# Gate and up of a SwiGLU as seven half products (Strassen) for 16 of 22 tiles, the down projection in five groups, and weights halved 1024 wide

## The chip, the cores and the metric

The kernel runs on one core of one Trainium2 chip, in one launch. The metric is the device time in microseconds, the median of several runs. The engines of the core work side by side, each on its own queue in order: TensorE (PE) for matmuls into PSUM, with its weight loads (PEld), VectorE (DVE), ScalarE (ACT), GpSimd (POOL), and SyncE (SP), which issues the transfers.

## The reference

A trunk of two layers on a sequence of 512 tokens of 1024 features, float32. Each layer is a macaron:

```python
x = x + 0.5 * swiglu(rms_norm(x, ffn1_norm[i]), ...)      # width 2816
x = x + mixer(rms_norm(x, mix_norm[i]))                   # layer 0: block-sparse attention, layer 1: Mamba-2
x = x + 0.5 * swiglu(rms_norm(x, ffn2_norm[i]), ...)

def swiglu(x, w_gate, w_up, w_down):
    return (jax.nn.silu(x @ w_gate) * (x @ w_up)) @ w_down
```

So there are four SwiGLU blocks (FFNs 0 to 3) with gate and up of 1024 x 2816 and down of 2816 x 1024.

## The kernel before

Everything is kept transposed: `x` is eight tiles of 128 features x 512 tokens in SBUF, `h` (the hidden width) is 22 tiles of 128 x 512. Precision comes from halves: each operand a is split into a high part (rounded to the matmul's type by ScalarE, `high`) and a low part (a minus the high part, on VectorE, `low`), and each 128 x 128 block of a product is three matmuls, high by high, high by low, low by high (`mm3`). Names end in `hi` and `lo`: `whi`, `wlo` are halves of weights, `xhi`, `xlo` of the normed input, `hhi`, `hlo` of the hidden tiles.

Weights stream in through four raw buffers `wraw` of 128 x 2048 (1 MB), in the order of use. `halve_weights` cuts each into units of 512 columns and makes `whi` (ScalarE) and `wlo` (VectorE), with eight buffers of each kind; a unit is four 128 x 128 blocks, 12 matmuls of 512 columns.

An FFN (`ffn`) runs in two halves of 11 hidden tiles. In each half, for every tile j, a gate accumulation `pg` and an up accumulation `pu` over the eight tiles of x (48 matmuls, each in a PSUM bank of its own); then `gated` makes h from them: `pg` times the row norm `rb` (VectorE), silu (ScalarE), times `rb` (GpSimd), times `pu` (VectorE), and the halving of the result. After 11 tiles come eight down blocks `pd`, one for each tile of x, 33 matmuls each, and `residual` adds each to x on VectorE. The next stage's norm starts tile by tile as x is done (`Norm.add`): operands are scaled by the gain and halved at once, and the norm's row factor `rb` is applied later, in `gated`. The mixers use the same weights' machinery; in `wide`, used for q, k, v and z, two raw pieces (eight units) are held over two passes.

The order of work on all engines is not written by hand. A planner (`Scheduler`) runs the stages as tasks with its own costs for each operation; it issues next what could start first by its clock, with the priority as a tie break, so an instruction's place in its engine's queue is decided by these costs. The main task has the matmuls; the halving of weights is given as `EASY` work with a due time, and becomes `URGENT` when its due time is near (`pressing`). Buffers are pools (`slot` 128 x 512, `hs` 128 x 256, `ps` eight PSUM banks), given out by the planner.

Of the kernel before, what the change touches and what calls it, by code (L numbers as in the profile page):

```python
# [25 lines left out]
KT = D // 128  # L26
# [11 lines left out]


# [103 lines left out]
class Scheduler:  # L143
    def __init__(self, sizes):
# [3 lines left out]
        self.tag_of = {}  # L148
        self.written, self.read = {}, {}
# [82 lines left out]
    def release(self, tile):  # L232
        name = tile.tensor.name
        ends = [s[2] for book in (self.written, self.read) for s in book.pop(name, ())]
        room = self.room[self.tag_of.pop(name)]
        room.append(max(ends))
# [54 lines left out]
def trunk(ctx, tc, xT, pos, consts, cols, rows, wgu, wd, wqk, wv, wo, win, wz, wdt, wout, outT):  # L291
# [10 lines left out]
    sizes = {"slot": 48, "hs": 12, "sq": 6, "tiny": 40, "ps": 8, "wraw": 4, "whi": 8, "wlo": 8}  # L302
# [10 lines left out]
    raw_piece, hi_unit, lo_unit = room(wp, "wraw", 2048), room(wp, "whi", 512), room(wp, "wlo", 512)  # L313
# [24 lines left out]
    pieces = []  # L338

    def piece(src, n=2048, unit=2.73, total=None):  # L340


        pieces.append((src, n, unit, unit * n / 512 if total is None else total))

    def wide_pieces(w):
        piece(w[0], unit=1.36)
        piece(w[1], unit=1.36, total=16.4)

    for l in range(2):
        for i in (2 * l, 2 * l + 1):  # L350
            if i == 1:
                for what, c in ATTN:
                    if what == "wo":
                        piece(wo[c])
                    else:
                        wide_pieces(wqk[c] if what == "qk" else wv[c])
            if i == 3:
                piece(wdt, 256, total=5.5)
                for what, n in SSM:
                    if what == "x":  # L360
                        piece(win[n, 0])
                        piece(win[n, 1])
                    elif what == "z":
                        wide_pieces(wz[n])
                    else:
                        piece(wout[n, 0])
                        piece(wout[n, 1])
# [6 lines left out]
    needed = [0.0]  # L374
    for _, _, _, total in pieces:
        needed.append(needed[-1] + total)
    used = [0]

    def load_weights():
        for p in range(1, len(pieces)):  # L380
            src, n = pieces[p][:2]
            raw = yield raw_piece("wraw")
            yield SP.dma_start(raw[:, :n], src)
            raws[p], begun[p] = raw, n

    def halve_weights():
        for p in range(len(pieces)):
            n = pieces[p][1]
            cs = range(0, n, 512)
            for c in cs:  # L390
                at_work[:] = p, c
                yield When(lambda: begun.get(p, 0) > c)
                hi, lo = yield [hi_unit("whi", FR), lo_unit("wlo", FR)]
                w = min(512, n - c)
                yield high(raws[p][:, c:c + w], hi[:, :w])
                spawn(halve_low(p, c, w, hi, lo, c == cs[-1]), pressing(p, c))

    def halve_low(p, c, w, hi, lo, last):
        op = low(raws[p][:, c:c + w], hi[:, :w], lo[:, :w])
        yield op.frees(raws.pop(p)) if last else op  # L400
        units.setdefault(p, []).append((hi, lo))
# [3 lines left out]
    def pressing(p, c):  # L405

        due = needed[p] + c / 512 * pieces[p][2]
        return lambda: URGENT if due - Q.done_us < 6.0 else EASY + due

    def first_due():  # L410
        p, c = at_work
        return pressing(p, c)()
# [4 lines left out]
    def take(src):  # L417
        p = used[0]
        used[0] += 1
        assert pieces[p][0].offset == src.offset and pieces[p][0].tensor.name == src.tensor.name  # L420
# [753 lines left out]
```

## Time and profile before

| | us |
|---|---|
| median of 3 runs | 2116.16 (2116.1 to 2117.05) |
| the profiled execution | 2115.9 |
| its span on the core | 2113.9 |
| TensorE busy | 2106.1 |
| VectorE busy | 1117.0 |
| ScalarE busy | 877.6 |
| GpSimd busy | 400.4 |

How to read it: the span is the time from the first to the last instruction of the profiled execution, which is 0.3 us off the median of the runs. Busy time is the union of an engine's instructions. In the groups, a row has the line of the helper that records every operation (L214), the engine, the operation, output and inputs by the program's names, the shapes, the count, the busy time, the mean duration in ns of one, and the idle time of the engine before them with what ended it. A matmul's duration has its drain in it, which overlaps the next matmul; so its cost is the distance between starts. In windows, each engine has its busy time in that stretch and its number of instructions.

### The profile page before, as it was taken

What the parts mean: (1) busy time and instruction counts of PE and PEld (TensorE: products, weight loads), DVE (VectorE), ACT (ScalarE), POOL (GpSimd) and SP (SyncE); (2) the same over time, 40 slices, a digit from 0 to 9 for tenths busy, and PEclk for the clock granted to TensorE, in tenths of its full rate; (3) what the DMA queues carried; (4) which work ended last, traced back from release to release, by engine and by line L of the source; (5) the groups of instructions that cost most, each with busy time, mean ns of one, the idle gap of its engine ahead of it and who ended that gap; (6) DMA issues with size and microseconds to landing.
All of it is one profiled execution on the core that took longest, in us unless ns stands there. A gap on an engine that the chain in (4) does not pass through costs nothing.

```text
span 2113.9 us, 25353 instructions
## 1 busy us (share of the span) xinstructions
PE 2106.1 (100%) x9700; PEld 1748.7 (83%) x9700; DVE 1117.0 (53%) x1841; ACT 877.6 (42%) x1650; POOL 400.4 (19%) x377
## 2 busy tenths in 40 slices
PE   9999999999999999999999999999999999999999
PEld 7888888888888888888888888888888888888887
DVE  6444444668864434444443444677575774443442
ACT  5322334455443323333322334674747643322331
POOL 1101111332131001111100111244343442100100
PEclk9999999999999999999999999999999999999999
DMA  6223223212122232232232223233232332232221
GB/s 229 81 96 110 96 83 114 100 60 80 60 81 87 92 114 95 83 110 98 81 108 100 94 83 116 81 84 136 68 132 69 112 117 83 81 109 101 93 87 49
DMA packets 37129, 203.68 MB, mean 96 GB/s; under 512 B 4240, under 2 KB 4880, under 8 KB 19728
## 3 DMA queue, kind: packets, MB, share of 16 engines
q1 hardware_dynamic: 37008, 202.07, 27.9%
q8 instruction: 76, 1.25, 0.2%
q14 instruction: 45, 0.37, 0.1%
HBM read 199.89 MB, written 2.16 MB: 96 GB/s over the span
## 4 chain that ended last, share of the span: by engine, by line
PE 98%; DMA 1%; DVE 0%; ACT 0%; SPq 0%; POOL 0%; issue 0%; ACTq 0%; POOLq 0%
PE pd L214 23%; PE pu L214 22%; PE pg L214 22%; PE pin L214 8%; PE pqk L214 4%; PE pz L214 4%; PE pout L214 4%; PE pv L214 2%; PE pwo L214 2%; PE py L214 2%; PE psc L214 1%; PE pxt L214 1%; PE po L214 1%; PE pst L214 1%; PE ppt L214 0%; DMA wraw<-wgu 0%
## 5 line engine op out<-in xcount | busy, mean ns | idle before, releaser
L214 DVE TENSOR_TENSOR wlo<-wraw,whi 128x512 fp32r<-128x512 f32 (+1 forms) x737 | 555.3, 759 | 677.5 <-ACT whi L214 668.6
L214 ACT ACTIVATE whi<-wraw 128x512 fp32r<-128x512 f32 (+1 forms) x737 | 453.1, 619 | 778.7 <-PE pd L214 281.2
L214 POOL TENSOR_TENSOR ga<-ga,rb 128x512 f32<-128x512 f32 x88 | 114.1, 1298 | 977.8 <-ACT ga L214 575.0
L214 PE MATMUL pg<-xhi,whi 128*128 128x512 f32 x704 | 274.3, 390 | 1.2 <-ACT xhi L214 1.2
L214 PE MATMUL pg<-xlo,whi 128*128 128x512 f32 x704 | 274.2, 390 | 0.5 <-DVE xlo L214 0.5
L214 PE MATMUL pu<-xhi,whi 128*128 128x512 f32 x704 | 274.4, 390 | 0.0
L214 PE MATMUL pg<-xhi,wlo 128*128 128x512 f32 x704 | 273.9, 389 | 0.0
L214 PE MATMUL pu<-xhi,wlo 128*128 128x512 f32 x704 | 273.9, 389 | 0.0
L214 PE MATMUL pu<-xlo,whi 128*128 128x512 f32 x704 | 273.9, 389 | 0.0
L214 PE MATMUL pd<-hhi,whi 128*128 128x512 f32 x704 | 273.9, 389 | 0.0
L214 PE MATMUL pd<-hlo,whi 128*128 128x512 f32 x704 | 273.9, 389 | 0.0
L214 PE MATMUL pd<-hhi,wlo 128*128 128x512 f32 x704 | 273.9, 389 | 0.0
L214 PEld LDWEIGHTS pg<-xlo,whi 128*128 128x128 f32 x704 | 132.2, 188 | 29.0 <-DVE xlo L214 1.6
L214 PEld LDWEIGHTS pg<-xhi,whi 128*128 128x128 f32 x704 | 132.1, 188 | 28.9 <-ACT xhi L214 1.5
L214 PEld LDWEIGHTS pu<-xhi,wlo 128*128 128x128 f32 x704 | 132.2, 188 | 27.5
L214 PEld LDWEIGHTS pd<-hhi,wlo 128*128 128x128 f32 x704 | 132.1, 188 | 27.5
L214 PEld LDWEIGHTS pd<-hhi,whi 128*128 128x128 f32 x704 | 132.1, 188 | 27.4
L214 PEld LDWEIGHTS pu<-xhi,whi 128*128 128x128 f32 x704 | 132.2, 188 | 27.3
L214 PEld LDWEIGHTS pd<-hlo,whi 128*128 128x128 f32 x704 | 132.1, 188 | 27.4
L214 PEld LDWEIGHTS pg<-xhi,wlo 128*128 128x128 f32 x704 | 132.1, 188 | 27.3
L214 PEld LDWEIGHTS pu<-xlo,whi 128*128 128x128 f32 x704 | 132.1, 188 | 27.3
L214 ACT ACTIVATE hhi<-ga 128x512 fp32r<-128x512 f32 x88 | 55.6, 632 | 149.8 <-DVE ga L214 149.8
(211 smaller groups left out, 3036.4 us busy)
## 6 DMA issues: line engine op xcount, KB each, us to landing
wraw<-wgu SPq DMA_DIRECT2D x87, 1024.0 KB, 4.8
wraw<-wd SPq DMA_DIRECT2D x64, 704.0 KB, 4.1
wraw<-win SPq DMA_DIRECT2D x16, 1024.0 KB, 4.9
wraw<-wqk SPq DMA_DIRECT2D x8, 1024.0 KB, 4.9
wraw<-wz SPq DMA_DIRECT2D x8, 1024.0 KB, 4.9
rows_b<-rows_d SPq DMA_DIRECT2D x32, 256.0 KB, 5.5
wraw<-wout SPq DMA_DIRECT2D x8, 1024.0 KB, 4.8
wraw<-wv SPq DMA_DIRECT2D x4, 1024.0 KB, 4.8
```

The costliest lines, as they stand in the source:

```text
L214: op.fn(*op.args, **op.kw)
```

## The change

Six of the 22 hidden tiles stay as they were (`plain`), the other 16 are taken as 8 pairs. For a pair (j0, j1) the normed input is seen as a 2 x 2 matrix of blocks (A11, A12, A21, A22: tokens 0 to 255 and 256 to 511, features 0 to 511 and 512 to 1023) and the weights of the two tiles as another one (features by tile), and the four result blocks come from seven products in place of eight (Winograd's form of Strassen's scheme). Each product is 24 matmuls for gate and for up together: 4 blocks of features, three halves, twice, with 256 columns, gate in the left and up in the right half of one PSUM bank (`pp`). VectorE combines the products from PSUM (`c11`, `w_e`, `c12`, `c22`, `c21`), with the names `g1` to `g4`, and `gate` does the silu and the multiplication for 256 tokens.

The operands of the products are made in two places. `spread` makes the seven sums and differences of the normed input, once per FFN, with `rb` already applied (so in `gate` no factor `rb` is left and GpSimd has no part): `aa`, `ab`, `ad`, `ae` with their halves. `halve_pair` makes the seven sums of weights in place in the raw buffers (VectorE, 1024 columns: gate and up), and halves each.

The down projection goes by groups: (0, 6), (6, 10), (10, 14), (14, 18), (18, 22). Down blocks of a group are put among the pairs of the next group, four after each pair; each has 18 or 12 matmuls and its own `residual`. Weights are halved in units of 1024 columns, with four buffers of each kind; a unit that serves two accumulations is freed after both (`uses`).

```diff
+GROUPS = ((0, 6), (6, 10), (10, 14), (14, 18), (18, 22))
...
-    sizes = {"slot": 48, "hs": 12, "sq": 6, "tiny": 40, "ps": 8, "wraw": 4, "whi": 8, "wlo": 8}
+    sizes = {"slot": 55, "hs": 12, "sq": 6, "tiny": 40, "ps": 8, "wraw": 4, "whi": 4, "wlo": 4}
...
-    raw_piece, hi_unit, lo_unit = room(wp, "wraw", 2048), room(wp, "whi", 512), room(wp, "wlo", 512)
+    raw_piece, hi_unit, lo_unit = room(wp, "wraw", 2048), room(wp, "whi", 1024), room(wp, "wlo", 1024)
...
+    def ffn_order(i):
+
+        order = list(range(*GROUPS[0]))
+        for g in range(1, len(GROUPS)):
+            a, b = GROUPS[g]
+            pairs = [(j, j + 1) for j in range(a, b, 2)]
+            n = 0
+            for m, pair in enumerate(pairs):
+                order.append(pair)
+                while n < KT * (m + 1) // len(pairs):
+                    order.append(("down", g - 1, n))
+                    n += 1
+        return order + [("down", len(GROUPS) - 1, n) for n in range(KT)]
...
-            for hf in range(2):
-                for j in range(HALF):
-                    piece(wgu[i, hf * HALF + j])
-                for n in range(KT):
-                    piece(wd[i, hf, n], HALF * 128)
...
+            for c in range(0, n, 1024):
                 hi, lo = yield [hi_unit("whi", FR), lo_unit("wlo", FR)]
...
-                w = min(512, n - c)
+                w = min(1024, n - c)
...
+    def halve_pair(p, a, b):
+        a0, a1, b0, b1 = a[:, :1024], a[:, 1024:], b[:, :1024], b[:, 1024:]
+        plan = [(a0, None, []), (a0, b0, []), (a1, None, []), (a0, b1, []), (b1, None, []), (b0, b1, [b]), (a0, a1, [a])]
+        for m, (src, term, done) in enumerate(plan):
+            at_work[:] = p, m
+            if term is not None:
+                yield When(lambda: len(units[p]) == m)
+                yield V.tensor_tensor(src, src, term, op=OP.add)
+            hi, lo = yield [hi_unit("whi", FR), lo_unit("wlo", FR)]
+            yield high(src, hi)
+            spawn(halve_low(p, src, hi, lo, done), pressing(p, m))
...
-        return lambda: URGENT if due - Q.done_us < 6.0 else EASY + due
+        return lambda: URGENT if due - Q.done_us < 8.0 else EASY + due
...
+        def spread(self):
+            yield When(lambda: self.rb is not None)
+            rest = []
+            for k in range(4):
+                xa, xb = yield [slot("xa"), slot("xb")]
+                for t, kk in ((xa, k), (xb, k + 4)):
+                    op = V.scalar_tensor_tensor(t, x[kk], self.gain[:, kk:kk + 1], self.rb, op0=OP.mult, op1=OP.mult)
...
+                bh, bl, d = yield [slot("abhi", FR), slot("ablo", FR), slot("ad")]
+                yield high(xb, bh)
+                yield V.tensor_tensor(d[:, :256], xa[:, 256:], xb[:, 256:], op=OP.subtract)
+                yield low(xb, bh, bl)
+                yield V.tensor_tensor(d[:, 256:], xa[:, :256], d[:, :256], op=OP.subtract)
+                yield V.tensor_tensor(xb[:, :256], xb[:, :256], d[:, 256:], op=OP.subtract)
+                yield V.tensor_tensor(xb[:, 256:], xa[:, :256], xa[:, 256:], op=OP.subtract)
+                ah, al, dh, dl = yield [half_slot("aahi", FR), half_slot("aalo", FR), slot("adhi", FR), slot("adlo", FR)]
+                yield high(xa[:, :256], ah)
+                yield low(xa[:, :256], ah, al).frees(xa)
+                yield high(d, dh)
+                yield low(d, dh, dl).frees(d)
...
+            for k in range(4):
+                eh, el = yield [slot("aehi", FR), slot("aelo", FR)]
+                yield high(rest[k], eh)
+                yield low(rest[k], eh, el).frees(rest[k])
...
+            def product(m, name):
+                ps = yield bank("pp")
+                yield unit(p, m)
+                un = units[p][m]
+                for o in range(2):
+                    for k in range(4):
+                        yield When(lambda: nrm.left[name][k] is not None)
+                        ops = mm3(ps[:, 256 * o:256 * o + 256], cut(un, 512 * o + 128 * k, 512 * o + 128 * k + 128),
+                                  nrm.left[name][k], k == 0, k == 3)
+                        if o and k == 3:
+                            ops[-1].frees(*un)
+                        if last and o:
+                            ops[-1].frees(*nrm.left[name][k])
+                        yield ops
+                return ps
...
+            def gate(j, t, src):
+                if j not in out:
+                    out[j] = [None, 2]
+                    out[j][0] = yield slot("ga")
+                yield When(lambda: out[j][0] is not None)
+                a = out[j][0][:, 256 * t:256 * t + 256]
+                yield S.activation(a, src[:, :256], AF.Silu)
+                yield V.tensor_tensor(a, src[:, 256:], a, op=OP.mult).frees(src)
...
+            def c11(ps):
+                yield When(lambda: "P1" in st)
+                t = yield slot("g2")
+                yield V.tensor_tensor(t, ps, st["P1"], op=OP.add).frees(ps)
+                st["C11"] = t
+                yield from gate(j0, 0, t)
+            def w_e(p6, p5):
+                yield When(lambda: "C11" in st)
+                w = st["P1"]
+                yield V.tensor_tensor(w, p6, w, op=OP.subtract).frees(p6)
+                e = yield slot("g3")
+                yield V.tensor_tensor(e, p5, w, op=OP.add).frees(p5)
+                st["W"], st["E"] = w, e
...
+            def c22(ps):
+                yield When(lambda: "C12" in st)
+                w, e = st["W"], st["E"]
+                yield V.tensor_tensor(w, ps, w, op=OP.subtract)
+                st["D"] = w
+                yield V.tensor_tensor(e, e, ps, op=OP.subtract).frees(ps)
...
+            ps = yield from product(0, "A11")
+            spawn(p1(ps), 6)
+            p5 = yield from product(1, "A21-A22")
+            ps = yield from product(2, "A12")
+            spawn(c11(ps), 6)
+            ps = yield from product(3, "S2")
+            spawn(w_e(ps, p5), 6)
+            ps = yield from product(4, "A12-S2")
+            spawn(c12(ps), 6)
+            ps = yield from product(5, "A11-A21")
+            spawn(c22(ps), 6)
+            ps = yield from product(6, "A22")
+            spawn(c21(ps), 6)
+        def down(g, n):
+            p = take(down_src(i, n, g))
+            ps = yield bank("pd")
+            a, b = GROUPS[g]
+            for j in range(a, b):
...```

The operations that the built program has more or fewer of: gate and up matmuls of 512 columns, each of six groups, 704 to 192; matmuls of 256 columns for the products, 0 to 5376; residuals of `pd` 64 to 160; sums of raw weights 0 to 128; halvings of weights 736 to 530, of which 366 are 1024 wide; combinations of products 224; GpSimd's multiplications `ga` 88 to 24.

Three places in the order, with the numbers of buffers left in the names.

TensorE, before, in FFN 0 at the change from gate to up of one tile (`pg_695` and `pu_696` are the two banks):

```order
L214 MATMUL pg_695<-xhi_108,whi_566 128x512
L214 MATMUL pg_695<-xlo_109,whi_566 128x512
L214 MATMUL pg_695<-xhi_108,wlo_567 128x512
L214 MATMUL pu_696<-xhi_98,whi_584 128x512
L214 MATMUL pu_696<-xlo_99,whi_584 128x512
L214 MATMUL pu_696<-xhi_98,wlo_585 128x512
```

TensorE, changed, in the first pair of FFN 0 at the change from its first product (A11) to its second (A21-A22):

```order
L218 MATMUL pp_726<-aahi_637,whi_596 128x256
L218 MATMUL pp_726<-aalo_638,whi_596 128x256
L218 MATMUL pp_726<-aahi_637,wlo_597 128x256
L218 MATMUL pp_766<-adhi_381,whi_693 128x256
L218 MATMUL pp_766<-adlo_382,whi_693 128x256
L218 MATMUL pp_766<-adhi_381,wlo_694 128x256
```

The matmuls follow each other in threes in the same way, with 256 columns instead of 512 and a new weight unit after 24 of them, where it was after 12.

VectorE, before, one tile of gate and up in FFN 0 (`wraw_478` has the raw weights of a later tile):

```order
L214 TENSOR_TENSOR wlo_721<-wraw_478,whi_720 128x512
L214 TENSOR_TENSOR wlo_739<-wraw_478,whi_738 128x512
L214 TENSOR_TENSOR wlo_755<-wraw_478,whi_754 128x512
L214 TENSOR_TENSOR ga_774<-pg_695,rb_355 128x512
L214 TENSOR_TENSOR wlo_771<-wraw_478,whi_770 128x512
L214 TENSOR_TENSOR ga_774<-pu_696,ga_774 128x512
L214 TENSOR_TENSOR hlo_792<-ga_774,hhi_791 128x512
```

VectorE, changed, in a later pair of FFN 0 (`wraw_1574` and `wraw_1612` are the raw weights of its two tiles; `g2`, `g1` and `g3` are C11, then W, then E):

```order
L218 TENSOR_TENSOR wraw_1574<-wraw_1574,wraw_1612 128x1024
L218 TENSOR_TENSOR wlo_1764<-wraw_1574,whi_1763 128x1024
L218 TENSOR_TENSOR wlo_1783<-wraw_1612,whi_1782 128x1024
L218 TENSOR_TENSOR wraw_1612<-wraw_1612 128x1024
L218 TENSOR_TENSOR wlo_1819<-wraw_1612,whi_1818 128x1024
L218 TENSOR_TENSOR wraw_1574<-wraw_1574 128x1024
L218 TENSOR_TENSOR g2_1843<-pp_1813,g1_1781 128x512
L218 TENSOR_TENSOR g1_1781<-pp_1842,g1_1781 128x512
L218 TENSOR_TENSOR wlo_1857<-wraw_1574,whi_1856 128x1024
L218 TENSOR_TENSOR wlo_1878<-wraw_1643,whi_1877 128x512
L218 TENSOR_TENSOR ga_1869<-g2_1843,ga_1869 128x256
L218 TENSOR_TENSOR g3_1884<-pp_1784,g1_1781 128x512
```

The sums and halves of weights of the pair stand ahead of the first combination; the seventh unit's low half (`wlo_1857`) and the first down block's (`wlo_1878`) stand behind the subtraction for W, which needs the fourth product.

VectorE, before, in FFN 0 where the row norm is ready:

```order
L214 TENSOR_TENSOR wlo_331<-wraw_131,whi_330 128x512
L214 TENSOR_TENSOR ga_362<-pg_90,rb_355 128x512
L214 TENSOR_TENSOR wlo_360<-wraw_131,whi_359 128x512
L214 TENSOR_TENSOR ga_383<-pg_264,rb_355 128x512
L214 TENSOR_TENSOR wlo_380<-wraw_131,whi_379 128x512
L214 TENSOR_TENSOR ga_362<-pu_91,ga_362 128x512
```

VectorE, changed, at the same place:

```order
L218 TENSOR_TENSOR wlo_308<-wraw_131,whi_307 128x1024
L218 SCALAR_TENSOR_TENSOR xa_336<-x0_71,colp_79,rb_331 128x512
L218 SCALAR_TENSOR_TENSOR xb_337<-x4_75,colp_79,rb_331 128x512
L218 TENSOR_TENSOR ga_338<-pg_92,rb_331 128x512
L218 TENSOR_TENSOR ad_349<-xa_336,xb_337 128x256
L218 TENSOR_TENSOR ablo_348<-xb_337,abhi_347 128x512
L218 TENSOR_TENSOR ad_349<-xa_336,ad_349 128x256
L218 TENSOR_TENSOR xb_337<-xb_337,ad_349 128x256
L218 TENSOR_TENSOR xb_337<-xa_336 128x256
L218 TENSOR_TENSOR ga_362<-pg_255,rb_331 128x512
```

The first round of `spread` stands between the gatings of the first two tiles, where low halves of weights stood.

More of the change, by code (lines that the diff above doesn't have):

```diff
@@ L373, in trunk @@
+            for what in ffn_order(i):
+                if isinstance(what, int):
+                    job([wgu[i, what]])
+                elif what[0] == "down":
+                    job([down_src(i, what[2], what[1])])
+                else:
+                    job([wgu[i, j] for j in what], step=2.88, total=20.2)
     raws, begun, units = {}, {}, {}
-    needed = [0.0]
-    for _, _, _, total in pieces:
-        needed.append(needed[-1] + total)
     used = [0]
     def load_weights():
[L380 to L384, printed above, removed]
@@ new lines, in halve_low @@
+    def halve_low(p, src, hi, lo, done):
+        yield low(src, hi, lo).frees(*done)
+        w = src.free_size()
+        for c in range(0, w, 512) if len(jobs[p][0]) == 1 else (0,):
+            b = w if len(jobs[p][0]) == 2 else min(c + 512, w)
+            units[p].append((hi[:, c:b], lo[:, c:b]))
+    def halve_pair(p, a, b):
[9 more added lines that the diff above has]
+            spawn(halve_low(p, src, hi, lo, done), pressing(p, m))
@@ L473, in __init__ @@
             self.added = 0
+            self.plain, self.spread_left = 2 * GROUPS[0][1], 8
+            self.left = {nm: [None] * 4 for nm in ("A11", "A12", "A22", "A21-A22", "S2", "A12-S2", "A11-A21")}
         def add(self, k, first=False):
@@ L543, in ffn, with halve, gated @@
         spawn(nrm.finish(), 20)
-        left = [NH]
-        def gated(pg, pu, h, j):
+        spawn(nrm.spread(), 60)
+        h = {}
+        def halve(a, j):
+            hi, lo = yield [slot("hhi", FR), slot("hlo", FR)]
+            yield high(a, hi)
+            yield low(a, hi, lo).frees(a)
+            h[j] = (hi, lo)
+        def gated(pg, pu, j):
             yield When(lambda: nrm.rb is not None)
@@ new lines, in gated, with plain @@
+            op = GP.tensor_tensor(a, a, nrm.rb, op=OP.mult)
+            nrm.plain -= 2
+            yield op.frees(*([] if nrm.plain or nrm.spread_left else [nrm.rb]))
+            yield V.tensor_tensor(a, pu, a, op=OP.mult).frees(pu)
+            yield from halve(a, j)
+        def plain(j, last):
+            p = take(wgu[i, j])
+            pg, pu = yield [bank("pg"), bank("pu")]
+            for u in range(2):
+                for o, ps in ((0, pg), (1, pu)):
+                    yield unit(p, 2 * u + o)
+                    un = units[p][2 * u + o]
+                    for kk in range(4):
+                        k = 4 * u + kk
+                        yield When(lambda: nrm.h[k] is not None)
+                        ops = mm3(ps, cut(un, 128 * kk, 128 * kk + 128), nrm.h[k], k == 0, k == KT - 1)
+                        if kk == 3:
+                            ops[-1].frees(*un)
+                        if last and o == 1:
+                            ops[-1].frees(*nrm.h[k])
+                        yield ops
+            spawn(gated(pg, pu, j))
@@ L596, in trunk @@
+        for what in ffn_order(i):
+            if isinstance(what, int):
+                yield from plain(what, what == GROUPS[0][1] - 1)
+            elif what[0] == "down":
+                if midway and what[1] == 2 and what[2] == 0:
+                    midway()
+                yield from down(*what[1:])
+            else:
+                yield from pair(*what, what == (NH - 2, NH - 1))
     tabs = []
@@ L1110 @@
             wgu[i, j] = np.concatenate([pack(w, ks, cols_of(j)) for ks in (lo4, hi4) for w in (wg, wu)], axis=1)
-        for hf in range(2):
-            for n in range(KT):
-                wd[i, hf, n] = pack(wn, slice(hf * HALF, hf * HALF + HALF), cols_of(n))
+        for n in range(KT):
+            wd[i, n] = pack(wn, slice(0, NH), cols_of(n))
     qkv = inp["attn_w_qkv"][0]
```

180 lines of the change are left out of this document (102 added, 78 removed).

## The prediction

> **What bounds the kernel now.** I read the page first (busy times, the clock, the chain that ended last), then the waits of TensorE, then groups by form, then the timeline at the few places where 256-wide matmuls already run, then windows.
>
> ```profile
> PE 2106.1 (100%) x9700; PEld 1748.7 (83%) x9700; DVE 1117.0 (53%) x1841; ACT 877.6 (42%) x1650; POOL 400.4 (19%) x377
> ...
> PEclk9999999999999999999999999999999999999999
> ...
> PE 98%; DMA 1%; DVE 0%; ACT 0%; SPq 0%; POOL 0%; issue 0%; ACTq 0%; POOLq 0%
> ```
> ```profile
> PE pg L214 <- ACT xhi L214: 1.2, 1, 1.2
> PE warm L214 <- DVE warm L1054: 1.2, 1, 1.2
> ```
>
> TensorE is busy for 2106.1 of 2113.9 us at the full clock, the chain is 98% TensorE, and its longest waits are 1.2 us each. So only matmul time counts, and other engines count from the point at which they make TensorE wait. What one matmul is worth is not its duration in a group (390 ns, with a drain that overlaps the next) but its pitch, start to start:
>
> ```profile
> L214 PE MATMUL pg<-xhi,whi 128*128 128x512 f32 x704 | 274.3, 390 | 1.2 <-ACT xhi L214 1.2
> L214 PEld LDWEIGHTS pg<-xhi,whi 128*128 128x128 f32 x704 | 132.1, 188 | 28.9 <-ACT xhi L214 1.5
> ...
> 129.85 59.84 PE pd L214 x264
> ```
>
> The last row is a piece of the chain: 264 matmuls of 512 columns in 59.84 us, 226.7 ns each.
>
> **The matmuls.** The six gate and up groups go from x704 to x192 (16 of 22 tiles leave them, in four FFNs): 3072 matmuls of 512 columns are removed. In their place come 32 pairs with 7 products of 24 matmuls, 5376 of 256 columns. A pair costs 96 x 0.2267 = 21.76 us now. What it costs then hangs on one number, the pitch at 256 columns when every matmul has a new weight load. The attention already does this, three at a time:
>
> ```profile
> 418.70 0.36 PE L214 MATMUL psc<-qkhi 128*128 128x256 f32 x1
> 418.90 0.28 PE L214 MATMUL psc<-qklo,qkhi 128*128 128x256 f32 x1
> 419.02 0.28 PE L214 MATMUL psc<-qkhi,qklo 128*128 128x256 f32 x1
> 419.14 0.23 PE L214 MATMUL psc<-neg_b,ident_b 128*128 128x128 bf16 x1
> ```
> ```profile
> 433.87 0.34 PE L214 MATMUL po<-ptlo,vhi 128*128 128x384 f32 x1
> 434.04 0.34 PE L214 MATMUL po<-pthi,vlo 128*128 128x384 f32 x1
> 434.22 0.29 PE L214 MATMUL po<-pthi,vhi 128*128 128x256 f32 x1
> 434.35 0.28 PE L214 MATMUL po<-ptlo,vhi 128*128 128x256 f32 x1
> 434.47 0.29 PE L214 MATMUL po<-pthi,vlo 128*128 128x256 f32 x1
> 434.59 0.22 PE L214 MATMUL po<-pthi,vhi 128*128 128x128 f32 x1
> ```
> ```profile
> 434.47 0.19 PEld L214 LDWEIGHTS po<-pthi,vhi 128*128 128x128 f32 x1
> 434.59 0.19 PEld L214 LDWEIGHTS po<-ptlo,vhi 128*128 128x128 f32 x1
> 434.70 0.19 PEld L214 LDWEIGHTS po<-pthi,vlo 128*128 128x128 f32 x1
> ```
>
> In `psc` the starts after the first lie 0.12 apart; in `po` three take 0.37 us (434.22 to 434.59), 0.123 each. The step from 512 to 384 columns (0.2267 to about 0.175, from 433.87 to 434.22) is 0.052, which leads to 0.123 at 256 as well. The bounds are 0.115 (the 0.24 us of `psc` can be 0.23 before rounding) and 0.13 (the widest interval). I take 0.121, between the two means, nearer to `psc`, since the last interval of `po` leads to a narrower matmul. The third block says why it isn't bound by the loads: they follow each other at 0.12 and 0.11 us, so the recorded 0.19 overlaps the next one, and a load can come every 0.11. The margin to 0.121 is thin. A pair then takes 168 x 0.121 = 20.33 us, 1.43 us less; 32 pairs give -45.9 us. The ends are -78 us (0.115) and +3 us (0.13): the pitch at which nothing is won is 21.76 / 168 = 0.1295.
>
> The Trainium skill speaks against this: "TensorE: Matmul & The Clock Gate", section "The mechanism" of Part 3, says a weight load overlaps with running matmuls only when they use different row groups, and here each load fills all rows. The trace does not agree: at 512 columns a load that waits its turn would give 0.227 + 0.11, and the chain shows 0.2267. By the rule the sum would be that of the second rival below.
>
> **The down projection.** Its 2112 matmuls stay. They now go in five groups of 6 or 4 tiles, 160 accumulations instead of 64, so 96 more residual additions on VectorE, none on TensorE. The bytes are the same; the 704 KB transfers become 160 of 384 or 256 KB:
>
> ```profile
> wraw<-wgu SPq DMA_DIRECT2D x87, 1024.0 KB, 4.8
> wraw<-wd SPq DMA_DIRECT2D x64, 704.0 KB, 4.1
> ```
>
> A period (a pair and four down blocks) loads 3 MB in 31 us, 97 GB/s, as now. The next pair's two megabytes go into the raw buffers of the pair's first two down blocks, whose halves are done some 14 and 16 us into the pair (by the weight buffers, below). One after the other, at 4.8 us each, they have landed by 19 and 24; they are needed at 23 (after the first down block) and 26. Cost nothing; without that cover up to 5 us a period.
>
> **VectorE in the pair stages.** Prices of one instruction:
>
> ```profile
> L214 DVE TENSOR_TENSOR wlo<-wraw,whi 128x512 fp32r<-128x512 f32 x672 | 517.2, 776 | 588.0 <-ACT whi L214 579.2 <-PE pd L214 7.6
> L214 DVE TENSOR_TENSOR hlo<-ga,hhi 128x512 fp32r<-128x512 f32 x88 | 63.0, 716 | 58.0 <-ACT hhi L214 58.0
> L214 DVE TENSOR_TENSOR ga<-pg,rb 128x512 f32<-128x512 f32 x88 | 60.1, 683 | 3.1 <-ACT rb L214 1.9 <-PE pg L214 1.2
> L214 DVE SCALAR_TENSOR_TENSOR x<-pd,x 128x512 f32<-128x512 f32 x64 | 44.2, 691 | 70.1 <-PE pd L214 70.0
> L214 DVE SCALAR_TENSOR_TENSOR xlo<-x,colp,xhi 128x512 fp32r<-128x512 f32 x48 | 37.5, 794 | 6.5 <-ACT xhi L214 6.4
> L214 DVE TENSOR_TENSOR y<-py,dx 128x256 f32<-128x256 f32 x32 | 13.4, 420 | 12.3 <-PE py L214 12.3
> ...
> L214 ACT ACTIVATE whi<-wraw 128x512 fp32r<-128x512 f32 x672 | 419.2, 629 | 682.5 <-PE pd L214 218.1 <-PE pg L214 171.2 <-PE pu L214 154.7
> ...
> L214 POOL TENSOR_TENSOR ga<-ga,rb 128x512 f32<-128x512 f32 x88 | 114.1, 1298 | 977.8 <-ACT ga L214 575.0 <-PE pu L214 402.8
> ```
>
> From 0.691 at 512 and 0.420 at 256 columns (1.06 ns per column), 1024 columns take an estimated 1.23 us; the upper bound is two of the present ones, 1.4. A period on VectorE: 7 low halves and 4 sums of weights (11 x 1.23 = 13.5), 7 combinations of products (7 x 0.69 = 4.8), 4 half-width gatings (4 x 0.42 = 1.7), 2 halvings of h (1.4), and four times a low half and a residual (4 x 1.4 = 5.6): 27.0 us. TensorE needs 20.33 + 48 x 0.2267 = 31.2 us. VectorE is full to 87% (29 us with 1.4 per wide one, 93%) and does not bind. ScalarE is further off: 7 x 1.06 (estimated from 0.629 at 512 columns) and some nine short ones, 13.5 us.
>
> Order matters too. There are four weight buffers of 1024 where there were eight of 512: one freed at the end of a unit serves the fourth unit after it, so the halving has 3 units = 8.2 us (down blocks) or 8.7 us (products), where it had 7 x 2.72 = 19 us. It needs 1.06 + 1.23 = 2.3 us, so a queue of nearly 6 us on VectorE may stand ahead. The worst I find is the seventh unit: its low half stands behind the subtraction for W, which waits for the end of the fourth product (4 x 24 x 0.121 = 11.6 us), so it ends at about 13.5 and is needed at 17.4; behind it stand the first down block's low half (needed at 20.3) and the next combination, whose bank of eight is wanted later still. No stall; cost 0, price if the cover goes: about 1 us a pair. In the mixers, where all units of a `wide` are held over two passes, the time for the halving goes from 9.5 to 8.2 us: 0 as well. TensorE stood still there for 0.23 us at 82% VectorE:
>
> ```profile
> 500.00:600.00 100.00, 99.77 (x512) 82.75 (x512) 82.16 (x159) 56.62 (x138) 29.31 (x22) 1.00 0.18 64
> ```
>
> **The spread, at the head of each FFN.** It is new work on VectorE beside the six plain tiles, which take TensorE 288 x 0.2267 = 65.3 us. Each of four rounds has 2 scaled copies (0.79), 5 half-width ones (0.42) and 3 low halves (0.69): 5.8 us, 23 in all. The tiles need 6 x (2 x 1.23 + 2 x 0.68 + 0.72) = 27.2 us, the first units of the first pair 7.4: 58 us, 89%. GpSimd works in this stage, and there a low half takes 776 instead of 691 ns, 1.12 times: 65 us, just full. At 1.2 times the first pair comes 4 us late. So the stall is 0 to 4 us for each of four FFNs; I take 1 us, 4 in all.
>
> **Sum.** -45.9 + 4 = -42. The profiled execution took 2115.9 us (span 2113.9), the median of the runs is 2116.16; so 2074 us.
>
> **Rivals.**
> 1. VectorE sets the pace of the pair stages and the kernel becomes slower. A period is 32.6 us now (21.76 + 10.88); VectorE's 27.0 must grow 1.21 times for a loss. At 1.25 times it is 33.8, 1.1 us lost in 32 periods: 2152 us. For it: the mean of 776 ns shows that two-input work on VectorE can be drawn out. Against it: that is 1.12 times, and happens beside GpSimd, whose 64 `ga` multiplications of 1.3 us leave these stages; VectorE was 82% busy in the window above without cost.
> 2. The weight loads bind. If each took its recorded 0.188 us, a pair would take 31.6 us, +9.8, and the kernel 2431 us. If they did not overlap at all, a matmul would take 0.12 + 0.11, a pair 38.6, the kernel about 2656 us. This second form is what the rule of the Trainium skill above would do. Against it: the starts 0.12 apart. For it: only runs of three are seen.
> 3. Something between: the pitch over long runs is nearer 0.129, the gain is used up, 2114 to 2120 us.
> 4. The shorter lead of the weight buffers costs a microsecond a pair: 2074 + 32 = 2106 us, still faster.
>
> **How the numbers follow.** The forecast (2060 to 2090) has 78%, rival 4 has 8%, rival 3 has 5%, rival 1 has 5%, rival 2 has 4% (1% of it for the second form). A difference under 0.2% (4 us) is about what a measurement of this kernel cannot tell from none; so faster 86%, same 5%, slower 9%. The range: below, 0.120 with no stall gives 2065 and 0.118 gives 2054; above, rival 4. 2056 to 2106.
>
> **What would show it.** Right: the `pp` matmuls 0.12 us apart over a whole pair (168 in 20.3 us); TensorE's waits on `wlo` and `whi` under 10 us in all; VectorE at 75 to 80% of the span (a pair's 21.4 us without its down blocks, against two tiles of 4 x 0.71 + 2 x 0.68 + 0.72 = 4.9 now: 370 us more, 66 for residuals, 92 for the spread), 1024-wide low halves near 1.23 us; PEclk still 9. Wrong: starts of `pp` 0.13 apart or more (rivals 2 and 3), or gaps before `pp` that a weight half or a sum of raw weights releases, in every period (1 and 4), or only before the first pair of an FFN (the spread). If TensorE has no gaps and the time is still off, the pitch was mis-sized.

## The result, and the profile after

The changed kernel takes 2068.24 us (2067.97 to 2068.47, 4 runs), the kernel before it on the same chip 2116.29 us (2116.1 to 2117.05): ratio 0.9772, 95% interval 0.9755 to 0.9789. Forecast were 2074 us, 42 us less; measured are 48 us less. The profiled execution took 2068.2 us, with a span of 2066.4.

From its page: the busy times, the clock, and the chain that ended last.

```profile
PE 2057.4 (100%) x12004; PEld 1818.2 (88%) x12004; DVE 1559.6 (75%) x2243; ACT 967.8 (47%) x1604; POOL 340.8 (16%) x313
...
PEclk9999999999999999999999999999999999999999
...
PE 96%; DMA 1%; DVE 1%; ACT 1%; POOL 0%; issue 0%; SPq 0%; DVEq 0%; ACTq 0%
```

TensorE is still the whole chain. VectorE went from 53% to 75% of a shorter span, 443 us more, and is 1% of the chain. TensorE's waits (engine, tile waited for: total, times, longest):

```profile
PE pg L218 <- DVE xlo L218: 1.4, 3, 0.7
PE pg L218 <- ACT xhi L218: 1.3, 1, 1.3
PE warm L218 <- DVE warm L1250: 1.2, 1, 1.2
PE py L218 <- DVE M L218: 0.6, 1, 0.6
PE ptr L218 <- POOL ropea L218: 0.5, 1, 0.5
PE pwo L218 <- DVE qklo L218: 0.2, 1, 0.2
PE pg L218 <- DVE wlo L218: 0.2, 1, 0.2
```

No wait of `pp` or `pd` is in the list, which is whole here. Two pieces of the chain (start, length), and the first matmuls of a pair from the timeline:

```profile
76.19 20.15 PE pp L218 x168
96.34 16.35 PE pd L218 x72
```
```profile
211.14 0.28 PE L218 MATMUL pp<-aahi,whi 128*128 128x256 f32 x1
211.26 0.28 PE L218 MATMUL pp<-aalo,whi 128*128 128x256 f32 x1
211.38 0.28 PE L218 MATMUL pp<-aahi,wlo 128*128 128x256 f32 x1
```

Each of the 32 pairs takes 20.15 us: 168 matmuls, 119.9 ns from start to start. Before, the same work was 96 x 0.2267 = 21.76 us. A period of the pair stages (20.15 + 10.88) and the spread at the head of FFN 0, in windows (length, busy us of PE, PEld, DVE, ACT, POOL with counts, granted clock, DMA share, GB/s):

```profile
10.00:76.00 66.00, 65.84 (x293) 54.15 (x293) 58.67 (x87) 36.74 (x55) 9.43 (x7) 0.99 0.39 141
...
180.25:211.31 31.06, 31.06 (x218) 29.17 (x218) 25.27 (x33) 12.70 (x18) 0.00 (x0) 1.00 0.30 103
```

VectorE is 81% busy in this period (25.3 us, as in most of them; 27.9 in the busiest, 90%) and 89% in the spread. In the periods TensorE doesn't stop at all, in the spread for 0.16 us. VectorE's groups by form (busy us, mean ns | idle before):

```profile
L218 DVE TENSOR_TENSOR wlo<-wraw,whi 128x1024 fp32r<-128x1024 f32 x366 | 468.5, 1282 | 170.4 <-ACT whi L218 168.8
L218 DVE TENSOR_TENSOR wraw<-wraw 128x1024 f32<-128x1024 f32 x128 | 157.4, 1229 | 0.3
```

By stage, from the starts in the two traces: the pairs are worth 32 x (21.76 - 20.15) = 51.5 us, and the span fell by 47.5. The other 4.0 us were lost outside the pairs: 1.2 in FFN 1, 1.0 in FFN 0, 0.9 in the Mamba-2 mixer, 0.5 in the attention, 0.2 in each of FFNs 2 and 3. For the larger ones the trace names a wait that the kernel before doesn't have: in FFN 1 the first matmuls stand idle for 0.40 and 0.73 us until `xlo` is there (at 587.02 and 588.72), in the attention `ptr` waits for `ropea`, in the Mamba-2 mixer `py` for `M`. The last one differs from execution to execution: the mixer takes 432.5 us in this one, 431.6 in the kernel before, and 431.6 to 432.3 in the traces of the runs e1, e3 (with 7) and e4 to e9 below.

### The profile page after: what moved, and what is told of

It is laid out like the page before. It is cut to its first block, busy times and chain, and to the rows that moved or that the text cites. A ratio compares the mean times of both kernels' runs of the same rounds, so it can differ in the third digit from the quotient of the medians.

```text
span 2066.4 us, 30164 instructions
## 1 busy us (share of the span) xinstructions
PE 2057.4 (100%) x12004; PEld 1818.2 (88%) x12004; DVE 1559.6 (75%) x2243; ACT 967.8 (47%) x1604; POOL 340.8 (16%) x313
## 4 chain that ended last, share of the span: by engine, by line
PE 96%; DMA 1%; DVE 1%; ACT 1%; POOL 0%; issue 0%; SPq 0%; DVEq 0%; ACTq 0%
PE pp L218 31%; PE pd L218 23%; PE pin L218 7%; PE pu L218 6%; PE pg L218 6%; PE pz L218 4%; PE pout L218 4%; PE pqk L218 3%; PE pv L218 2%; PE pwo L218 2%; PE py L218 2%; PE psc L218 1%; PE po L218 1%; PE pxt L218 1%; DMA rows_b<-rows_d 1%; PE pst L218 1%
## 5 line engine op out<-in xcount | busy, mean ns | idle before, releaser
L218 ACT ACTIVATE whi<-wraw 128x1024 fp32r<-128x1024 f32 (+2 forms) x531 | 496.5, 938 | 737.0 <-DVE wraw L218 276.0
L218 DVE TENSOR_TENSOR wlo<-wraw,whi 128x1024 fp32r<-128x1024 f32 (+2 forms) x531 | 587.5, 1112 | 178.3 <-ACT whi L218 174.5
L218 PE MATMUL pd<-hhi,whi 128*128 128x512 f32 x704 | 274.3, 390 | 0.0
L218 PE MATMUL pd<-hlo,whi 128*128 128x512 f32 x704 | 274.3, 390 | 0.0
L218 PE MATMUL pd<-hhi,wlo 128*128 128x512 f32 x704 | 273.9, 389 | 0.0
L218 DVE SCALAR_TENSOR_TENSOR x<-pd,x 128x512 f32<-128x512 f32 x160 | 109.6, 689 | 81.5 <-PE pd L218 81.5
L218 POOL TENSOR_TENSOR acc<-acc,sq 128x512 f32<-128x512 f32 x35 | 51.0, 1457 | 693.9 <-ACT sq L218 693.5
L218 DVE TENSOR_TENSOR wraw<-wraw 128x1024 f32<-128x1024 f32 x128 | 157.4, 1229 | 0.3
L218 PEld LDWEIGHTS pd<-hhi,wlo 128*128 128x128 f32 x704 | 132.2, 188 | 27.5
L218 PEld LDWEIGHTS pd<-hhi,whi 128*128 128x128 f32 x704 | 132.3, 188 | 26.7
L218 PEld LDWEIGHTS pd<-hlo,whi 128*128 128x128 f32 x704 | 132.3, 188 | 26.3
L218 DVE TENSOR_TENSOR g<-pp,g 128x512 f32<-128x512 f32 x192 | 132.1, 688 | 28.3 <-PE pp L218 23.2
L218 PE MATMUL pp<-adhi,whi 128*128 128x256 f32 x512 | 144.9, 283 | 0.0
L218 PE MATMUL pp<-adlo,whi 128*128 128x256 f32 x512 | 144.9, 283 | 0.0
L218 PE MATMUL pp<-adhi,wlo 128*128 128x256 f32 x512 | 144.9, 283 | 0.0
L218 PE MATMUL pp<-abhi,whi 128*128 128x256 f32 x512 | 144.9, 283 | 0.0
L218 PE MATMUL pp<-ablo,whi 128*128 128x256 f32 x512 | 144.9, 283 | 0.0
L218 PE MATMUL pp<-abhi,wlo 128*128 128x256 f32 x512 | 144.9, 283 | 0.0
L218 PE MATMUL pp<-aehi,whi 128*128 128x256 f32 x512 | 144.9, 283 | 0.0
L218 PE MATMUL pp<-aelo,whi 128*128 128x256 f32 x512 | 144.9, 283 | 0.0
L218 PE MATMUL pp<-aehi,wlo 128*128 128x256 f32 x512 | 144.9, 283 | 0.0
L218 PE MATMUL pin<-xhi,whi 128*128 128x512 f32 x256 | 103.7, 405 | 0.0
```

Source lines behind the costliest of these rows:

```text
L218: op.fn(*op.args, **op.kw)
```

## The experiments

The theory (A): the time is the pitch of the matmuls, 168 at 0.120 against 96 at 0.2267 us, and all that was added on VectorE is hidden. Against it stand that part of the gain comes from the regrouping or the wider halving (B), that the weight loads bind or nearly bind (C), that VectorE nearly binds (D), and that the shorter lead of the weight buffers costs time (E).

### No products: e1_no_products

All 22 tiles as `plain`; the groups and the halving 1024 wide stay.

```diff
...
-        spawn(nrm.spread(), 60)
...
-                yield from pair(*what, what == (NH - 2, NH - 1))
+                for j in what:
+                    yield from plain(j, j == NH - 1)
```

> All 22 tiles of each FFN as plain tiles; the groups of the down projection, the 1024-wide halving and the buffers stay as changed. Theory A (the whole gain is the 32 pairs at 20.15 us instead of 21.76, 51.5 us, and the rest of the change costs 3 to 4 us): about 2116 to 2121 us. Rival B (groups and wider halving give a part of the gain): clearly under 2114 us. Under A VectorE falls back to about 55% of the span, since two low halves of 512 at 0.69 each become one of 1024 at 1.22.

Measured: 2118.12 us beside 2116.34, ratio 1.0008 (0.9999 to 1.0018). So regrouping and halving alone bring nothing (they cost 0 to 4 us), and B falls: the products are worth 2118.1 - 2068.2 = 49.9 us. TensorE has the same 9700 matmuls as before:

```profile
PE 2107.8 (100%) x9700; PEld 1748.7 (83%) x9700; DVE 1120.3 (53%) x1635; ACT 824.4 (39%) x1348; POOL 416.3 (20%) x377
```

By stage this kernel loses 1.0 us in FFN 1, 0.7 in FFN 0, 0.5 in the attention and 0.25 in the mixer against the kernel before. So about 2.4 of the 4.0 us lost outside the pairs are lost in the same stages without any product. The two waits for `xlo` in FFN 1 (0.39 and 0.73 us) and the one of `ptr` (0.5) are here too.

### Narrower matmuls: e2_128

Each product of 256 columns in two of 128: the same arithmetic, twice the weight loads.

```diff
-                for o in range(2):
+                for o, q in ((0, 0), (0, 128), (1, 0), (1, 128)):
...
```

> The products with 128 columns in each matmul, twice as many (336 a pair, each with its own weight load). Theory A (loads hidden, one every 0.11 us at most): a pitch of about 0.11, 37.3 us a pair, 17.2 more than 20.15, so about 2068 + 549 = 2617 us. If only columns and a fixed part counted (0.0135 + 0.0533 = 0.067 us): 22.4 us a pair, about 2141 us. If a load took its recorded 0.188 us: 63 us a pair, about 3440 us.

Measured: 2623.58 us in a single run. Two matmuls and their loads from the timeline:

```profile
100.09 0.27 PE L218 MATMUL pp<-aelo,whi 128*128 128x128 f32 x1
100.20 0.28 PE L218 MATMUL pp<-aehi,wlo 128*128 128x128 f32 x1
```
```profile
100.03 0.19 PEld L218 LDWEIGHTS pp<-aelo,whi 128*128 128x128 f32 x1
100.14 0.19 PEld L218 LDWEIGHTS pp<-aehi,wlo 128*128 128x128 f32 x1
```
```profile
75.07 37.47 PE pp L218 x336
```

336 matmuls in 37.47 us are 111.5 ns each (the last row is from the chain), hardly less than the 119.9 ns at twice the width. Half the columns should have saved some 52 ns, as the step from 512 to 384 did; it saved 8. So there is a floor of 111.5 ns with a new load for each matmul, and the 256-wide matmul lies 8 ns above it. At 256 columns the loads don't bind, though nearly: from 512 to 256 columns the distance falls by 106.8 ns, in proportion to the columns as from 512 to 384. At 128 something else than the columns sets it. That this is the load, which starts every 0.111 us there, is likely, but no run has such short matmuls without a new load. The recorded 0.19 us of a load is not its cost: the loads overlap each other and the matmuls.

### VectorE loaded on purpose: e3_burn7, e3_burn14

For each product one (or two) more instructions of 128 x 512 on VectorE, on a tile that nothing else uses: 7 or 14 a pair.

```diff
...
     def product(m, name):
...
+                spawn(burn(), 6)
...
+            def burn():
+                for _ in range(1):
+                    yield V.tensor_tensor(burnt, burnt, burnt, op=OP.max)
```

> Seven more VectorE instructions a pair, 128x512 with both inputs in SBUF on a tile of their own (one after each product is begun, about 0.7 us each, 4.9 us a pair). Theory A (VectorE has slack: 25.3 to 26.3 of 31.06 us busy in the periods of the changed kernel): 30 to 31 us of 31.06, so 0 to 10 us more, 2068 to 2078. By the prediction's sum of single durations (27.0 + 4.9 = 31.9 against 31.06): 24 full periods x 0.8 = 20 us more, 2088. Rival B (the order leaves no slack, any new VectorE work shows): 32 x 4.9 = 157 us more, 2225.

> Fourteen such instructions a pair (9.8 us). Theory A: 35.2 of 31.06 us in the 24 full periods, so VectorE sets the pace: 4.1 x 24 = 98 us more, less what the longer stretches beside the first two pairs and the last down blocks take up: 2130 to 2170 us, around or above the time of the kernel before; this is the point of the prediction's first rival. Rival B: 32 x 9.8 = 314 us more, 2382.

Measured: 2071.96 us with 7 (ratio 0.979, 0.977 to 0.981), 2207.61 with 14 (1.0431, 1.041 to 1.0452). TensorE's waits of `pd` with 7, then windows: a period with 7, a period and a longer stretch with 14; then TensorE's longest wait with 14:

```profile
PE pd L218 <- ACT hhi L218: 1.3, 1, 1.3
...
PE pd L218 <- DVE hlo L218: 1.1, 1, 1.1
```
```profile
180.00:211.06 31.06, 31.06 (x218) 29.17 (x217) 28.59 (x38) 12.18 (x17) 0.00 (x0) 1.00 0.29 102
```
```profile
180.00:211.06 31.06, 31.06 (x218) 29.16 (x217) 28.79 (x39) 12.40 (x17) 0.00 (x0) 1.00 0.27 95
...
300.00:360.00 60.00, 55.49 (x342) 49.14 (x340) 53.60 (x80) 20.25 (x31) 0.00 (x0) 0.94 0.29 88
```
```profile
PE pd L218 <- ACT hhi L218: 78.9, 12, 13.2
```

With 7 more, VectorE is 92% busy in the period shown, and by the starts in the trace only one of the 32 periods is longer, the first of FFN 0 (41.4 us for 36.5): there TensorE waits 2.4 us for hidden tiles, at 99.9 and 101.95, and its clock falls (0.91 granted from 96 to 115 us). The other three FFNs agree with the changed kernel to 0.02 us. So D is false as it stands, a reserve of 3.3 us in an ordinary period costs nothing to use, and the first place where it ends is just behind the spread.

With 14 more, VectorE's work is about 25.3 + 14 x 0.6 = 33.7 us for a period of 31.06. Only 24 of the 32 periods are that short (the other 8, with down blocks of 18 matmuls, take 36.5), so 2.6 us over in each would give 2131, or 2152 if all 32 were; 2207 was measured. But VectorE doesn't fill up in the period shown: it is busy for 28.8 us, hardly more than with 7, TensorE has no gap there, and what isn't done is put off. It shows in a few places (spans 2204.6 and 2066.4): TensorE idles 95 us more, 79 us of it in twelve long waits of `pd` for hidden tiles, three in each FFN, the longest of 13.2 us among its last eight down blocks; and TensorE's busy time grows by 43 us, with a lower clock after such waits (granted 0.94 in the longer window).

### Other order, longer lead: e4_pairs_first

Both pairs of a group, then the eight down blocks.

```diff
-                while n < KT * (m + 1) // len(pairs):
+                while m + 1 == len(pairs) and n < KT:
```

> In each group the two pairs first and then the eight down blocks of the group before, instead of four after each pair. Two pairs on end need 2 x 21.4 = 42.8 us of VectorE by single durations, some 40 us with what overlaps, in 40.3 us of TensorE, with a lead of four weight buffers. Theory A (only the average over a group counts, the lead of 8 us covers the rest): 2066 to 2072 us. Rival C (the place of the down blocks among the pairs is needed, since the weights of a pair are made in one chain of some 20 us): 1 to 3 us for each of 16 groups, 2084 to 2116 us.

Measured: 2066.95 us, ratio 0.9767 (0.9753 to 0.978). From its chain:

```profile
210.75 40.31 PE pp L218 x336
```

336 matmuls at 120.0 ns without a gap, 14 units of 1024 columns in a row and no down block to catch up in. No wait of `pp` is in this run's list, nor in the changed kernel's, so the lead of the buffers (E) costs nothing in the pairs. Whether it has a part in the 2.4 us that e1 lost elsewhere was not tried.

### The head of FFN 0: e5_warm

Soon after 6.6 us in the profiled execution of the changed kernel TensorE falls to half clock; in that of the kernel before, at the same place, it does not. Timelines of after, then of before (in brackets the idle time):

```profile
6.56 0.51 PE L218 MATMUL pg<-xhi,whi 128*128 128x512 f32 x1 [1.31 <-ACT xhi L218]
...
8.09 0.63 PE L218 MATMUL pg<-xhi,whi 128*128 128x512 f32 x1
8.51 0.63 PE L218 MATMUL pg<-xlo,whi 128*128 128x512 f32 x1
```
```profile
6.64 0.50 PE L214 MATMUL pg<-xhi,whi 128*128 128x512 f32 x1 [1.23 <-ACT xhi L214]
...
7.76 0.40 PE L214 MATMUL pg<-xhi,wlo 128*128 128x512 f32 x1
7.99 0.40 PE L214 MATMUL pg<-xhi,whi 128*128 128x512 f32 x1
```

The matmuls lie 0.427 us apart where they lay 0.235 apart. The edit lengthens the warm-up that precedes them, `WARM = 22` to `WARM = 36`.

> 36 warm-up matmuls instead of 22 (14 more of 0.109 us, into the 1.6 us in which TensorE waits for the first input). In the changed kernel eight of the first matmuls run at 0.427 instead of 0.227 us after that wait, as at half the clock; in the kernel before they did not. Theory D (the wait lets the clock fall): 1.6 to 2 us less, 2066.5 us. Rival (it is something of the first transfers, or chance of a run): no difference, 2068.2.

Measured: 2066.86 us (2066.68 to 2066.91), ratio 0.9766 (0.9752 to 0.9779); the same kernel once more, on another chip:

> The kernel of e5 again, beside e8 on the same chip: 2066.7 to 2066.9 us, every pair 20.15 us, no stretch at half clock.

It gave 2067.48 us (2067.22 to 2068.14), ratio 0.9771 (0.9757 to 0.9784). Neither execution has a stretch at half clock. But the 1.4 and 0.8 us less than the changed kernel are not shown to come from that. By the starts in the traces, FFN 0 ends 0.6 us earlier in the first execution (356.6 us), and in the second at 357.2 as in the changed kernel, because its first matmuls wait for `xlo` and weights instead; in both, 0.75 us lie in the Mamba-2 mixer, where the changed kernel's wait of `py` for `M` is missing. And of the changed kernel's four runs only the profiled one has a mean granted clock of 0.999, the others 1.000, and their times are the same (2068.2 against 2067.97 to 2068.47). So the stretch at half clock belongs to that execution, as far as the mean clocks show, and the 1.6 to 2 us that theory D gave it are not borne out: by the traces at most 0.6 us can be the head's.

### More pairs: e6_nine, e7_nine_two, e8_nine_both, e9_nine_early

Each further pair should give 1.61 us. e6 takes nine pairs in each FFN, four plain tiles only, with four down blocks ahead of the first pair:

```diff
-GROUPS = ((0, 6), (6, 10), (10, 14), (14, 18), (18, 22))
+GROUPS = ((0, 4), (4, 8), (8, 12), (12, 16), (16, 22))
+AHEAD = 4
...
         def down(g, n):
+            yield When(lambda: not nrm.spread_left)
```

The last line is one more difference: the planner places no down block before the spread's scaled copies of the input are placed.

> Nine pairs in each FFN and four plain tiles; four down blocks of the first group stand ahead of the first pair, to give the spread its time. Theory A (matmul time alone): 4 x 1.61 = 6.4 us less, 2062 us. If the spread (23 us of VectorE) does not fit into 4 plain tiles and four down blocks (54.4 us of TensorE, about 54 us of VectorE by single durations), 1 to 4 us an FFN are lost again: 2064 to 2078 us.

Measured: 2084.91 us, ratio 0.9852 (0.9839 to 0.9866), 16.7 us worse than eight pairs. The place in FFN 0, from the timeline, and two windows there:

```profile
64.31 0.79 PE L219 MATMUL pd<-hhi,whi 128*128 128x512 f32 x1 [8.20 <-ACT hhi L219]
...
65.63 0.63 PE L219 MATMUL pd<-hhi,wlo 128*128 128x512 f32 x1
66.06 0.63 PE L219 MATMUL pd<-hhi,whi 128*128 128x512 f32 x1
```
```profile
55.00:64.00 9.00, 1.12 (x5) 0.58 (x4) 8.97 (x16) 4.87 (x10) 2.26 (x1) 0.79 0.15 48
64.00:70.00 6.00, 5.69 (x13) 4.18 (x14) 3.88 (x6) 1.92 (x3) 0.00 (x0) 0.50 0.00 0
```

VectorE is full (8.97 of 9 us) with the spread, the hidden tiles wait behind it, and TensorE with them; then it runs at half clock. Whether the added line has a part in that order was not tried. The spread ended 56 us after the start of FFN 0, 49 in FFN 1, but 39 in FFNs 2 and 3. So e7 takes nine pairs in FFNs 2 and 3 alone, with the long warm-up and the down blocks after the pairs (`GROUPS_OF = (SIX, SIX, FOUR, FOUR)`):

> Nine pairs (four plain tiles) in FFNs 2 and 3 alone, down blocks after pairs as in the changed kernel, and 36 warm-up matmuls. In the run with nine pairs everywhere, the spread of FFNs 2 and 3 was done 39 us after their start, within the 43.5 us of four plain tiles, while in FFN 0 it took 56 us; its loss came from down blocks that waited for the hidden tiles of the plain ones, which here come 20 us later. Theory A: 2066.9 (with the warm-up) less 2 x 1.61 = 2063.6 us. If the first pair has to wait for its operands or weights after all: 1 to 3 us for each of the two FFNs, 2065 to 2070 us.

Measured: 2071.15 us (2069.38 to 2071.84), ratio 0.9789 (0.9776 to 0.9802): 4.3 us slower than eight pairs with the same warm-up (e5), a miss. Its waits name `pd` again. e8 moves those down blocks behind both pairs (e4's edit on e7), 20 us later:

> Nine pairs in FFNs 2 and 3 as in e7, but both pairs of a group ahead of its eight down blocks, so the first group's hidden tiles are asked for 20.2 us later. If e7 lost its gain only because the down blocks of the first group waited for hidden tiles of the plain tiles, those waits vanish and the time is e5's 2066.9 less 2 x 1.61 = 2063.6 us, with TensorE's waits on hhi and hlo under 0.3 us in the profile. Rival: VectorE is behind by more than those 20 us, or the debt moves to the weight halves: then waits on wlo, g or aelo appear in place of them and the time stays at 2066 to 2071.

Measured: 2075.08 us (2073.19 to 2077.24), ratio 0.9807 (0.9794 to 0.9821), a miss again: the waits moved with the down blocks and grew. TensorE's waits in e7, then in e8:

```profile
PE pd L220 <- DVE hlo L220: 2.5, 3, 1.2
PE pd L220 <- ACT hhi L220: 1.7, 1, 1.7
```
```profile
PE pd L220 <- ACT hhi L220: 4.9, 2, 2.6
PE pd L220 <- DVE hlo L220: 2.1, 2, 1.9
```

In e8 VectorE even idled shortly before the wait, for 0.36, 0.53 and 0.66 us, while hidden tiles were still to be made, which speaks for order and against capacity. The code has it: `spawn(gated(...))` names no rank, so a plain tile's gating and halving get the planner's default, 100 and more. Of what could start at the same time, the pairs' combinations (6), the residuals (5), the spread (60) and pressing weight halves (-1) go first. e9 is e7 with one line added and one changed, which give them the combinations' rank once the spread is done:

```diff
-            spawn(gated(pg, pu, j))
+            late = lambda: 6 if nrm.left["A11-A21"][3] else 99 + 0.01 * j
+            spawn(gated(pg, pu, j), late if i >= 2 else None)
```

> e7 (nine pairs in FFNs 2 and 3, half of the down blocks after each pair) with one change: from the end of the spread on, the four plain tiles' gating and halving of h stand ahead of the weight halves that are not yet pressing, in the order of VectorE and ScalarE, where in e7 and e8 they came last. If the order was at fault and not VectorE's capacity, the waits of pd on hhi and hlo in FFNs 2 and 3 fall under 0.5 us and the time is 2063.6 to 2065 us (2 x 1.61 under e5's 2066.9 to 2067.5). If VectorE is simply full there (21.05 of 22 us busy in e7 before the stall), the debt only moves: gaps then stand before pp, released by wlo or g, and the time stays at 2067 to 2073.

Weight halves that are not yet pressing have a rank of 100000 and more, behind the plain tiles in e7 and e8 already; so what the edit moves is the tiles' place against the pairs' own work.

Measured: 2064.19 us (2063.91 to 2065.29), ratio 0.9756 (0.9743 to 0.977): 7.0 us faster than e7 and 4.0 faster than the changed kernel, the fastest of all. By the traces 2.7 are the two pairs (FFN 2 takes 346.24 us where it took 347.82, FFN 3 350.55 where it took 351.69); the rest lies in FFN 0 (1.0) and the Mamba-2 mixer (0.5). No wait on `hhi` or `hlo` is left. VectorE's queue just before the first down blocks of FFN 2, in e7 and in e9:

```profile
1000.93 1.89 DVE L220 TENSOR_TENSOR hlo<-ga,hhi 128x512 fp32r<-128x512 f32 x3
1002.74 0.68 DVE L220 TENSOR_TENSOR ga<-pu,ga 128x512 f32<-128x512 f32 x1
1004.12 0.69 DVE L220 TENSOR_TENSOR hlo<-ga,hhi 128x512 fp32r<-128x512 f32 x1 [0.69 <-ACT hhi L220]
```
```profile
990.91 0.68 DVE L220 TENSOR_TENSOR hlo<-ga,hhi 128x512 fp32r<-128x512 f32 x1
...
994.55 0.69 DVE L220 TENSOR_TENSOR hlo<-ga,hhi 128x512 fp32r<-128x512 f32 x1
```

and the windows there, e7 and then e9:

```profile
978.00:1000.00 22.00, 22.00 (x177) 21.66 (x176) 21.05 (x27) 10.55 (x17) 3.58 (x2) 1.00 0.25 92
1000.00:1006.00 6.00, 3.00 (x11) 1.64 (x10) 4.49 (x9) 2.56 (x5) 0.00 (x0) 1.00 0.47 191
```
```profile
978.00:1000.00 22.00, 22.00 (x177) 21.66 (x176) 20.95 (x27) 10.64 (x16) 4.06 (x2) 1.00 0.30 107
1000.00:1006.00 6.00, 6.00 (x28) 4.96 (x27) 5.78 (x9) 2.71 (x5) 0.00 (x0) 1.00 0.34 135
```

In e7 the last plain tile's multiplication by `pu` stands at 1002.74 and its `hlo` at 1004.12; in e9 that `hlo` is at 994.55. In the first window VectorE does the same 21 us of work in both. Only which of it came first differs, and TensorE stands still for 3 of the next 6 us or not at all.

## Why the prediction was right

**The pitch** carried the forecast, and was a little too high: 0.1199 us over whole pairs, taken as 0.121. This is the term that was mis-sized: -45.9 us forecast, -51.5 measured, inside the bounds of 0.115 and 0.13. The 0.123 of `po` and the doubt about 0.13 came from runs of three matmuls between others of different width; over 168 in a row the shorter interval of `psc`, 0.12, is the true one. That the spread's 4 us, which did not come, are made up by 4.0 us lost elsewhere is luck; so nearly the whole miss of 6 us is the pitch's.

**The weight loads** (rival 2) don't bind. The rule of the Trainium skill that the prediction weighed ("TensorE: Matmul & The Clock Gate", section "The mechanism" of Part 3) would have given 2656 us; the trace does not agree, neither at 119.9 ns nor in e2, where full-width loads for every matmul come every 111.5 ns. The same section also lets a load into a background weight buffer go ahead of running matmuls; the prediction weighed its closing line alone. The margin that the prediction called thin is 8 ns.

**VectorE** was forecast 27.0 us a period with a row for each instruction's duration; the window has 25.3 busy, the busiest period 27.9. The wide low half was right (1.23 estimated, median 1.225), but instructions in a row overlap: a subtraction that lasts 0.69 us is followed after 0.60, so durations overstate a full queue by 0.085 us each. e3 puts the point of rival 1 between 7 and 14 more instructions, 29.5 and 33.7 us by this count, and the prediction's 27.0 x 1.21 = 32.7 lies between. Its price was too low: 2152 at 1.25 times, 2207 measured. It took VectorE to be full when it sets the pace, while it was busy for 28.8 of 31.06 us, and it left out that the backlog shows as a few long waits, after which the clock falls.

**The lead of the buffers**, 8.2 us, cost nothing, as forecast. For the seventh unit's low half the working gave an end at 13.5 us into the pair; in the pair at 211.14 the trace has it at 224.7, 13.5 us, needed at 17.3. Rival 4 is refuted by the 32 pairs without a gap, and again by e4.

**The spread** was to cost 1 us for each FFN, 4 in all, before the first pair. It cost none there: in FFN 0 the last of its low halves ends at 68.8 us and the first pair starts at 76.2, with no wait before `pp` anywhere. VectorE's share in it, 89%, is as worked out, but in part by chance: the window holds 8.4 us of the norm's own work (`acc`, `xlo`) that the sum left out, and the last two plain tiles' multiplications by `pu` come after it. The 776 ns by which the working stretched the low halves is the mean over the whole kernel before, not that of this stage.

**What was missing**: the 4.0 us lost outside the pairs. They lie elsewhere than the 4 us of the spread, and 2.4 of them are lost in e1 too. That nothing is lost in the mixers was wrong by 1.4 us in this execution, by 0.6 in those of e5_warm and e5_again, which lack the wait for `M`. With pitch and spread put right and these losses left out the sum would have been 2116 - 51.5 = 2064.5.

## What to carry to other kernels

Where TensorE is the whole chain, price a scheme that trades matmuls for additions by pitch from start to start at the new width, over a long run with a new weight load each time: seven products of 256 columns beat eight only because 0.120 us is under 0.1295, and at 128 columns the same scheme costs 500 us. Then count the other engine's reserve per period, and load it on purpose to see where it ends: here it was never busy for more than some 95% of a period (30.2 of 31.7 us with 14 instructions more), and beyond that point the loss was larger than the overrun. And when a busy engine makes the bound one wait, look at which of its work stands first in its queue before calling it full: one change of priority turned a loss of 4.3 us into a gain of 2.7.

## What the runs showed of the hardware that was not expected

A wait of TensorE can cost more than itself. After idling 8.2 us (e6) it runs 0.427 us from start to start, granted clock 0.50 for 6 us; in the changed kernel the same follows an idle time of 1.31 us at 6.56 and lasts some 3.4 us. The length alone does not decide: 1.23 us at the same place in the kernel before brought no fall, while two waits of 1.1 and 1.3 us close together with 7 more instructions (e3) did (0.91 from 96 to 115 us), and two such waits in e7, the longer of 1.73 us, did not (granted clock 1.00 in its window above, and its matmuls 0.23 us apart after it):

```profile
1004.14 0.50 PE L220 MATMUL pd<-hhi,whi 128*128 128x512 f32 x1 [1.73 <-ACT hhi L220]
...
1005.20 0.39 PE L220 MATMUL pd<-hhi,wlo 128*128 128x512 f32 x1
1005.43 0.40 PE L220 MATMUL pd<-hhi,whi 128*128 128x512 f32 x1
```

The Trainium skill, "TensorE: Matmul & The Clock Gate", section "What's actually happening", says that a free-running window of about 3.4 us decides on the clock; the stretch of 3.4 us and the lack of a fixed length agree with that. Its advice to avoid gaps of over about 3 us (section "Why this matters for your kernels") doesn't cover this case, where 1.31 us sufficed once. What exactly the clock goes by was not tried and stays open. It does go with the spread of the times: the runs of e7 lie 2.5 us apart, the fastest (2069.38) with a mean granted clock of 1.000 and the slowest (2071.84) with 0.998, those of e8 4.1 us apart with 0.999 to 0.997, while all five of e5_warm have 1.000 and lie 0.2 apart. That suggests that the same waits are followed by a lower clock in some executions of one kernel and not in others; only one trace of each was kept.
